# Chunk preparation of a delta-net kernel: loads one chunk ahead, the prompt chunk first, block inverses woven into the next group

## The chip, the core and the metric

The kernel runs on one core of one Trainium2 chip. A core has five engines that run side by side, each through its own instructions in order: TensorE (PE in the profile; the loading of its stationary operand is listed as PEld), VectorE (DVE), ScalarE (ACT), GpSimd (POOL) and SyncE (SP). SyncE issues most of the transfers; ScalarE and POOL issue some. All transfers run on the same 16 DMA engines. The metric is the device time of one execution in microseconds (us).

## The reference

One layer of a flow-matching backbone, for 128 prompt tokens and 2048 sample tokens of width 1024. Both groups go through the same steps, with other modulation vectors:

```
xn   = rmsnorm(h, ln_g) * (1 + scale) + shift
proj = xn @ w_in            # q,k,v | beta, decay | z_a | u_b v_b | z_b | x_c | z_c | 3 gates
A: q,k,v = silu(short_conv(qkv)); q,k normalised per head
   o = gated_delta(forward) + gated_delta(backward);  o_a = rmsnorm(o) * silu(z_a)
B: vs = w_spatial[g] @ rmsnorm(v_b) + b_spatial   per block of 128 tokens;  o_b = u_b * vs * silu(z_b)
C: o_c = real(fft over the token grid and channels of x_c) * silu(z_c)
merged = sum over n of sigmoid(gate_n) * (o_n @ w_branch[n])
y    = rmsnorm(h + gate * (merged @ w_out), final_g)
```

The gated delta rule is S_t = a_t (I - b_t k_t k_t^T) S_(t-1) + b_t k_t v_t^T with o_t = S_t^T q_t. It is computed by chunks: within a chunk a unit lower triangular matrix I + N, with N = beta * (k k^T) * decay, has to be inverted, and between chunks a state is carried. The final states of the prompt are an output as well.

## The kernel before

Activations lie in SBUF as `xh` and `xl`, two float16 parts of the normalised input, so a product with a weight takes three matmuls (`gemm_T`, `gemm_N`, all recorded under the helper's line L160). Weights are fetched with `getw`, whose second argument is how many further weights are requested at once: a request is a load of 512 KB on SyncE's queue (`wst`, L183), a sum of squares on ScalarE (L187), a broadcast of it by TensorE (`wscb` times `ones`, L170), and a split into `whi` and `wlo` (L189, L190).

The stages of the main line, in order: adaptive modulation and normalisation; 12 column tiles of q, k, v with the short convolution, each stored to DRAM as `qkv` (L509 and after); B's first part, 17 token tiles of `v_b` with its spatial product (L868 to L885), stored as `vs`; B's second part, 4 groups of columns of `u_b` and `z_b` (L888 to L898, with `gate_unit`, L835 to L849), each over 5 blocks of tokens; C, the Fourier branch, 4 groups (L911 to L968); then the merges of branches B, C and A, each with its gates, and the output projection.

Beside this main line runs the delta branch A as a Python generator, `delta()`. `Pace.tick` adds up the main line's matmul time and, for every 1.6 us of it, runs the generator up to its next `yield`. So the order of the instructions is written by this weaving, and a scheduler then places them on the engines. `delta()` first prepares the chunks, then runs the two scans (`scan_dir`, with `level`).

There are 17 chunks of 128 tokens; chunk 16 is the prompt. `prep` (L540 to L594) does one chunk in 7 steps: it loads q, k and v of all heads (`qr` and `kq`, L544), transposes them on TensorE (L546), normalises (L550 to L558), stores k and v (`kv`, L560), transposes k again to `T` (L564), loads the decay matrices (`dc`, L569), forms N for both directions (L577) and stores it (L583), cuts out its 32 x 32 diagonal blocks on POOL (`nd`, L579) and stores them (L585), and forms the q k^T product (L588 to L592).

The diagonal blocks of a group of chunks are inverted together by `base_inverse` (L596 to L633): 8 loads (L608), 31 pairs of VectorE operations (L616, L617), a split in two float16 parts, and 16 stores (`es` on L632, `ei` on L630). Before, the groups are chunks 0-3, 4-7, 8-11, 12-15 and 16 alone, and each group's inverse follows its last chunk. The scan's `level` loads what these stores wrote (`sn`, `ec`, `e3` on L639 to L643) and masks it on POOL (L649, L652).

Nearly all of these transfers are on SyncE's queue, in which an instruction that waits holds those behind it. The buffers `tok`, `qr`, `dc`, `T`, `XB`, `E` and `Et` exist once, `kq`, `nd` and `n` twice.

Of the kernel before, what the change touches and what calls it, by code (L numbers as in the profile page):

```python
# [15 lines left out]
ALU = mybir.AluOpType  # L16
# [94 lines left out]
def hybrid_flow_kernel(ctx: ExitStack, tc: tile.TileContext, x_prompt, x_sample, state_delta, c, c_ctx, ln_g, w_ada,  # L111
# [410 lines left out]
    GROUPS = [list(range(0, 4)), list(range(4, 8)), list(range(8, 12)), list(range(12, 16)), [16]]  # L522
# [11 lines left out]
    def h3(ap):  # L534
        return ap.rearrange("p (h x) -> p h x", h=H)

    def prep(g, ci, t):
        tok = sb(dq, [P, 2, WB], "tok")
        qr = sb(dq, [P, H, P], "qr")
        ss = sb(dq, [P, 2, H], "ss2", bufs=2)  # L540
        for part in range(3):
            ps = bank(ps_d, [P, WB])
            kq = qr if part == 0 else sb(dq, [P, H, P], "kq", bufs=2)
            SY.dma_start(kq, qkvD[part * 4:part * 4 + 4, :, chunk_off(t):chunk_off(t) + P].rearrange("h p t -> p h t"))  # L544
            for h in range(H):
                PE.transpose(ps[:, hs(h)], kq[:, h, :], ident)  # L546
            if part == 2:
                A.copy(tok[:, 1, :], ps)
                continue
            sq = sb(dq, [P, WB], "sq")  # L550
            A.activation(sq, ps, AF.Square)
            V.tensor_reduce(ss[:, part, :], h3(sq), AX.X, ALU.add)
            G.tensor_scalar(ss[:, part, :], ss[:, part, :], EPS, None, ALU.add)
            G.tensor_tensor(ss[:, part, :], ss[:, part, :], mhalf.to_broadcast([P, H]), ALU.pow)
            if part == 0:
                G.tensor_scalar(rq[:, t, :], ss[:, 0, :], P ** -0.5, None, ALU.mult)
            else:
                V.tensor_tensor(h3(tok[:, 0, :]), h3(ps), bc(ss[:, 1, :], P), ALU.mult)  # L558
            yield 1
        SY.dma_start(kvD[t], tok)  # L560
        T = sb(dq, [P, WB], "T")
        ps = bank(ps_d, [P, WB])
        for h in range(H):
            PE.transpose(ps[:, hs(h)], tok[:, 0, hs(h)], ident)  # L564
        A.copy(T, ps)
        A.dma_start(kTD[t], T)
        yield 1
        dc = sb(dq, [P, 2, WB], "dc")
        SY.dma_start(dc, decD[t])  # L569
        ps = bank(ps_d, [P, WB])  # L570
        for h in range(H):
            mm(ps[:, hs(h)], T[:, hs(h)], T[:, hs(h)])
        nd = sb(dq, [P, 2, H, 32], "nd", bufs=2)
        for d in range(2):
            n_ = sb(dq, [P, WB], "n32", bufs=2)
            for h in range(H):
                V.scalar_tensor_tensor(n_[:, hs(h)], ps[:, hs(h)], beta[:, d, t, h:h + 1], dc[:, d, hs(h)], ALU.mult, ALU.mult)  # L577
            for B in range(4):
                G.tensor_copy(nd[32 * B:32 * B + 32, d], h3(n_)[32 * B:32 * B + 32, :, 32 * B:32 * B + 32])  # L579
            n16 = sb(dq, [P, 2, WB], "n16", F16, bufs=2)  # L580
            A.activation(n16[:, 0, :], n_, AF.Copy, scale=FS)
            V.scalar_tensor_tensor(n16[:, 1, :], n_, FS, n16[:, 0, :], ALU.mult, ALU.subtract)
            SY.dma_start(nD[d][t], n16)  # L583
            yield 1
        SY.dma_start(ndD[g][:, :, ci].rearrange("d p h i -> p d h i"), nd)  # L585
        ps = bank(ps_d, [P, WB])
        for h in range(H):
            mm(ps[:, hs(h)], T[:, hs(h)], qr[:, h, :])  # L588
        for d in range(2):
            q_ = sb(dq, [P, WB], "n32", bufs=2)  # L590
            V.tensor_mul(q_, ps, dc[:, d, :])
            SY.dma_start(qkD[d][t], q_)  # L592
            yield 1

    def base_inverse(g):
        nt = len(GROUPS[g])  # L596
        nb = 4 * nt
        X = sb(dq, [P, 2048], "XB")[:, 0:1024]
        E = sb(dq, [P, 1024], "E")
        tmp = sb(dq, [P, 1024], "Et")  # L600
        if nt < 4:
            V.memset(X, 0.0)
            V.memset(tmp, 0.0)
        b3 = lambda t_: t_.rearrange("p (j i) -> p j i", j=32)
        blk = lambda t_, d, B: b3(t_[d * 64 + B * 16:d * 64 + B * 16 + nb, :])
        for d in range(2):
            for B in range(4):
                SY.dma_start(blk(X if d == 0 else tmp, d, B), ndD[g][d, 32 * B:32 * B + 32].rearrange("j t h i -> (t h) j i"))  # L608
        V.tensor_copy(b3(X[64:P, :]), tmp[64:P, :].rearrange("p (i j) -> p j i", j=32))
        G.memset(E, 0.0)  # L610
        G.memset(E[:, 0:1024:33], 1.0)
        X3, E3 = b3(X), b3(E)
        for k in range(31, 0, -1):
            n_ = 32 - k
            t3 = tmp[:, 0:k * n_].rearrange("p (j i) -> p j i", j=k)
            V.tensor_tensor(t3, X3[:, 0:k, k:k + 1].to_broadcast([P, k, n_]), E3[:, k:k + 1, k:32].to_broadcast([P, k, n_]), ALU.mult)  # L616
            V.tensor_tensor(E3[:, 0:k, k:32], E3[:, 0:k, k:32], t3, ALU.subtract)  # L617
            if k % 2 == 0:
                yield 1
        V.tensor_copy(b3(tmp), E.rearrange("p (i j) -> p j i", j=32))  # L620
        yield 1
        e16 = sb(dq, [P, 32, 2, 2, 32], "XB", F16)
        for w_, src in enumerate((E, tmp)):
            A.activation(e16[:, :, w_, 0, :], b3(src), AF.Copy, scale=FS)
            V.scalar_tensor_tensor(e16[:, :, w_, 1, :], b3(src), FS, e16[:, :, w_, 0, :], ALU.mult, ALU.subtract)
        yield 1
        for d in range(2):
            for B in range(4):
                p0_ = d * 64 + B * 16
                SY.dma_start(eD[g][d, 32 * B:32 * B + 32].rearrange("j t h c -> (t h) j c"),  # L630
                             e16[p0_:p0_ + nb].rearrange("p j w l c -> p j (w l c)"))
                SY.dma_start(e32D[g][d, 32 * B:32 * B + 32].rearrange("j t h c -> (t h) j c"), blk(E if d == 0 else tmp, d, B))  # L632
        yield 1  # L633

    def level(d, t):
        g = min(t // 4, 4)
# [179 lines left out]

    def delta():
        nonlocal dq
        for g, ts in enumerate(GROUPS):
            for ci, t in enumerate(ts):  # L820
                yield from prep(g, ci, t)
            yield from base_inverse(g)
        dl.close()
        dq = pool(dl, "dqb", 1, side="right")
        for d in range(2):
            V.tensor_tensor(eg[:, d], eg[:, d], rq, ALU.mult)
        for d in range(2):
            yield from scan_dir(d)
        dl.close()
        dps.close()  # L830
# [23 lines left out]
    bp = pool(bs, "bp", 2)  # L854
    bsp = sb(bp, [P, 4, P], "bsp", bufs=1)
    SY.dma_start(bsp, b_spatial[0].rearrange("g (o p) -> o g p", o=1).to_broadcast([P, 4, P]))
    vw = getw(4, 1)
    wsT = sb(bp, [P, 4, P], "wsT", bufs=1)
    wsn = sb(bp, [P, 4, P], "wsn", bufs=1)
    SY.dma_start(wsn, w_spatial[0].rearrange("g p q -> p g q"))  # L860
    ps = bank(ps_x, [P, 4, P])
    for g in range(4):
        PE.transpose(ps[:, g, :], wsn[:, g, :], ident)
# [4 lines left out]
    for t in range(NCH):  # L868
# [16 lines left out]
        SY.dma_start(vsD[:, :, t * P:(t + 1) * P].rearrange("g p t -> p g t"), vs)  # L885
        pace.tick(5.2)
    bs.close()
    for g in range(4):  # L888
        uw, zw = getw(2, 2)
        for ti, (t0, tn) in enumerate(TBS):  # L890
            st = sb(ep, [P, tn], "st", bufs=3)
            SY.dma_start(st, vsD[g][:, t0:t0 + tn])
            ps = bank(ps_mm, [P, tn])
            gemm_T(ps, uw, 0, xh[:, :, t0:t0 + tn], xl[:, :, t0:t0 + tn])
            with tc.high_priority():
                V.scalar_tensor_tensor(st, ps, uw.inv, st, ALU.mult, ALU.mult)
            pace.tick(tn / 100)
            gate_unit(1, g, ti, zw, st)  # L898


    fs = ExitStack()
    fp = pool(fs, "fp", 1)
    cf = sb(fp, [P, _CW - _CF], "cf")
    SY.dma_start(cf, consts[:, _CF:_CW])
    for n_, (a, b) in _COFF.items():
        if a >= _CF:
            K[n_] = cf[:, a - _CF:b - _CF]
# [3 lines left out]
    for g in range(4):  # L911
        xw, zw = getw(2, 2)
        for gh in range(1):
            yT = sb(fp, [P, NTOK], "yT", bufs=1)
            Y1 = sb(fp, [P, 64, 32], "Y1")
            for q in range(0, NCH, 4):
# [13 lines left out]
                else:  # L930
# [1 line left out]
                    mm(ps, xc[:, 0, :], K["dftcs"])  # L932
                    yp = sb(fp, [P, 2 * P], "yp")
                    V.tensor_copy(yp, ps)
# [222 lines left out]
```

## Time and profile before

| what | value |
|---|---|
| device time, median of 3 runs | 2378.42 us (2374.1 to 2380.57) |
| profiled execution: device time | 2377.82 us |
| profiled execution: span | 2376.0 us |
| mean granted TensorE clock | 0.981 |
| TensorE busy | 2261.1 us (95%) |
| VectorE busy | 1271.6 us (54%) |
| ScalarE busy | 765.0 us (32%) |
| POOL busy | 820.9 us (35%) |
| moved by DMA | 350.40 MB, mean 147 GB/s |

The profile is that of one execution. Busy times are per engine and overlap each other. Rows of waits read "engine, operation and its line, what it waited for: total us, how often, the longest". SPq is SyncE's queue, whose rows are the issues of transfers and not the transfers. The granted clock (PEclk) is the speed that TensorE was given, as a share of full speed. In a group of instructions, "out<-in" names tiles without their buffer numbers; a `b` is a PSUM bank. "+15 forms" says that instructions of other shapes are in the same group.

### The profile page before, as it was taken

The numbers are of one execution on the slowest core, as the hardware profiler recorded it, in microseconds if no ns is written. First come the engines' busy times: TensorE is split into PE (matmuls) and PEld (weight loads), VectorE is DVE, ScalarE is ACT, GpSimd is POOL, SyncE is SP. The second block draws the span as 40 slices with busy tenths as digits, with TensorE's granted clock in tenths as the row PEclk, the third lists the DMA queues.
The fourth block names the chain that finished last, engine by engine and source line by source line (L and its number), as shares of the span: only waits on it lengthen the run. The fifth ranks groups of instructions, "written<-read, shape, count | busy, mean of one in ns | idle before, by whom it ended". The sixth has DMA issues, their size and how long they took to land. (4 is left out here: it accounts for less than half of the span.)

```text
span 2376.0 us, 43430 instructions
## 1 busy us (share of the span) xinstructions
PE 2261.1 (95%) x17092; PEld 1376.6 (58%) x17092; DVE 1271.6 (54%) x3117; ACT 765.0 (32%) x1430; POOL 820.9 (35%) x1056
## 2 busy tenths in 40 slices
PE   7999899998989987899989999999999999999998
PEld 3554444798545676679656656656665444444443
DVE  5635743568575856655574556674654242332453
ACT  3444543322333332332332222242332242221331
POOL 2421122342434431345423233445552212122543
PEclk9999999999999998999999999999999999999999
DMA  8315632375857672244453445565563253332542
GB/s 278 129 50 174 226 110 76 109 254 132 241 138 237 190 181 58 82 139 131 138 181 124 129 138 158 162 201 178 160 182 109 95 163 119 113 97 80 189 151 98
DMA packets 353238, 350.40 MB, mean 147 GB/s; under 512 B 70929, under 2 KB 273674, under 8 KB 351498
## 3 DMA queue, kind: packets, MB, share of 16 engines
q1 hardware_dynamic: 338986, 294.13, 41.9%
q0 software_dynamic: 9152, 40.13, 4.3%
q10 hardware_dynamic: 4896, 13.37, 1.5%
q8 instruction: 134, 2.20, 0.4%
q14 instruction: 70, 0.57, 0.1%
HBM read 222.16 MB, written 125.39 MB: 146 GB/s over the span
## 5 line engine op out<-in xcount | busy, mean ns | idle before, releaser
L160 PE MATMUL b<-xh,whi 128*128 128x512 f16 (+1 forms) x2080 | 707.2, 350 | 18.5 <-ACT raw L500 11.6
L160 PE MATMUL b<-xl,whi 128*128 128x512 f16 (+1 forms) x2080 | 708.5, 350 | 0.1
L160 PE MATMUL b<-xh,wlo 128*128 128x512 f16 (+1 forms) x2080 | 707.8, 350 | 0.0
L160 PEld LDWEIGHTS <-whi 128*128 128x128 f16 x4160 | 389.9, 98 | 402.0 <-issue 36.3
L160 PEld LDWEIGHTS <-wlo 128*128 128x128 f16 x2080 | 204.4, 98 | 195.8 <-issue 9.8
L160 PE MATMUL b<-big,bhi 128*128 128x512 f16 (+1 forms) x960 | 252.8, 348 | 5.7 <-ACT big L987 4.2
L1019 POOL TENSOR_TENSOR mrow<-mrow,sg 128x512 f32<-128x512 f32 (+1 forms) x80 | 87.9, 1102 | 317.0 <-DVE sg L1018 237.3
L160 PE MATMUL b<-whi,xh 128*128 128x128 f16 x1088 | 191.7, 222 | 0.6 <-DVE sg L844 0.5
L160 PE MATMUL b<-whi,xl 128*128 128x128 f16 x1088 | 191.8, 222 | 0.0
L160 PE MATMUL b<-wlo,xh 128*128 128x128 f16 x1088 | 191.8, 222 | 0.0
L160 PEld LDWEIGHTS <-xh 128*128 128x128 f16 x2312 | 179.5, 99 | 6.6 <-issue 5.8
L1009 ACT ACTIVATE sg<-b,winv 128x512 f32<-128x512 f32 (+1 forms) x120 | 74.6, 621 | 305.4 <-PE b L160 296.9
L160 PE MATMUL b<-big,blo 128*128 128x512 f16 (+1 forms) x480 | 163.8, 348 | 0.0
L1018 DVE SCALAR_TENSOR_TENSOR sg<-b,binv,sg 128x512 f32<-128x512 f32 (+1 forms) x80 | 53.5, 669 | 182.6 <-PE b L160 180.6
L752 POOL TENSOR_SCALAR skn<-skn,ed 128x128 f32<-128x128 f32 x136 | 80.5, 607 | 180.4 <-DMA skn<-kv 164.6
L160 PEld LDWEIGHTS <-bhi 128*128 128x128 f16 x960 | 89.2, 98 | 84.2 <-ACT big L987 2.4
L509 POOL TENSOR_TENSOR cy<-cy,raw 128x545 f32<-128x545 f32 (+1 forms) x48 | 55.4, 1180 | 223.6 <-ACT raw L508 223.6
L160 PEld LDWEIGHTS <-xl 128*128 128x128 f16 x1224 | 115.0, 99 | 0.4
L652 POOL TENSOR_TENSOR R<-ec,cst 128x512 f16<-128x512 f16 x68 | 72.6, 1088 | 103.6 <-PE b L160 50.5
L160 PE MATMUL b<-wohi,mh 128*128 128x512 f16 x272 | 104.2, 383 | 2.2 <-ACT mh L1064 2.2
L160 PE MATMUL b<-wohi,ml 128*128 128x512 f16 x272 | 104.1, 384 | 2.0 <-DVE ml L1065 2.0
L160 PE MATMUL b<-wolo,mh 128*128 128x512 f16 x272 | 104.2, 383 | 0.0
(369 smaller groups left out, 3714.9 us busy)
## 6 DMA issues: line engine op xcount, KB each, us to landing
wst<-in_w_in_dram SPq DMA_DIRECT2D x60, 512.0 KB
qkv<-cy POOLq DMA_DIRECT2D x12, 1089.0 KB, 4.5
mrow<-br SPq DMA_DIRECT2D x24, 512.0 KB
mrow<-mrg SPq DMA_DIRECT2D x19, 512.0 KB
mrow<-mrg SPq DMA_DIRECT2D x16, 576.0 KB
mrg<-mrow POOLq DMA_DIRECT2D x16, 576.0 KB, 3.2
dc<-dec SPq DMA_DIRECT2D x17, 512.0 KB
kq<-qkv SPq DMA_DIRECT2D x34, 256.0 KB
```

The costliest lines, as they stand in the source:

```text
L160: PE.matmul(out, l, r, start=start, stop=stop)
L509: G.tensor_tensor(y[:, c0:c1], y[:, c0:c1], raw[:, 1 + c0:1 + c1], ALU.mult)
L652: G.tensor_tensor(dst[:, l].rearrange("p h a b c -> p h (a b) c"), wide(ec[:, :, which ^ d, l, :]), bm, ALU.mult)
L752: G.tensor_scalar(kn_[:, hs(h)], kn_[:, hs(h)], ed[:, d, t, h:h + 1], None, ALU.mult)
L1009: A.activation(sg, ps, AF.Sigmoid, scale=gw.inv)
L1018: V.scalar_tensor_tensor(sg, ps, binv[:, 1:2], sg, ALU.mult, ALU.mult)
L1019: G.tensor_tensor(mr, mr, sg, ALU.add)
```

## The change

The order of the chunks becomes 16, then 0 to 15, with groups [16], 0-3, 4-7, 8-11, 12-15. `prep` no longer loads its own inputs: a dictionary `held` carries the k, v and q rows and the decay matrices of the next chunk, which each `prep` requests when its own last reader of that buffer has been issued. The order of the parts becomes k, v, q. The inverse of a group is stepped along with the preparation of the group after it, in five of each `prep`'s seven steps, and has five steps without work after its loads. The last group's inverse runs by itself, before the scans. The stores of `kv` and `nd` go from SyncE's queue to POOL's.

In the main line, B's spatial weights are requested before its first four weights. In B's second part, a whole row of `vs` (2176 tokens, 1.1 MB) is loaded for each group, one group ahead, in place of five blocks. The Fourier constants `cf` (640 KB) are loaded on ScalarE's queue instead of SyncE's. The second matrix product of the prompt's Fourier transform comes after the first of the four blocks of the sample's transform instead of before it.

```diff
-    GROUPS = [list(range(0, 4)), ..., list(range(12, 16)), [16]]
+    GROUPS = [[16], list(range(0, 4)), ..., list(range(12, 16))]
...
+    def rows(part, t):
+        x = sb(dq, [P, H, P], "kq" if part else "qr", bufs=2 if part else 1)
+        SY.dma_start(x, qkvD[part * 4:part * 4 + 4, :, chunk_off(t):chunk_off(t) + P].rearrange("h p t -> p h t"))
+        return x
...
-    def prep(g, ci, t):
+    def prep(g, ci, t, nxt, held):
...
+        cur = dict(held)
...
+        def more(key, make):
+            if nxt is not None:
+                held[key] = make()
+
+        ps = turned(1)
+        norm(ps, 1)
+        V.tensor_tensor(h3(tok[:, 0, :]), h3(ps), bc(ss[:, 1, :], P), ALU.mult)
+        yield 1
+        A.copy(tok[:, 1, :], turned(2))
+        more(1, lambda: rows(1, nxt))
+        norm(turned(0), 0)
+        G.tensor_scalar(rq[:, t, :], ss[:, 0, :], P ** -0.5, None, ALU.mult)
+        yield 1
+        G.dma_start(kvD[t], tok)
...
+        more(2, lambda: rows(2, nxt))
         yield 1
-        dc = sb(dq, [P, 2, WB], "dc")
-        SY.dma_start(dc, decD[t])
+        dc, qr = cur["dc"], cur[0]
...
-        SY.dma_start(ndD[g][:, :, ci].rearrange("d p h i -> p d h i"), nd)
+        G.dma_start(ndD[g][:, :, ci].rearrange("d p h i -> p d h i"), nd)
...
             SY.dma_start(qkD[d][t], q_)
+            if d:
+                more(0, lambda: rows(0, nxt))
+                more("dc", lambda: decay_rows(nxt))
             yield 1
...
     def base_inverse(g):
...
+        for _ in range(5):
+            yield 0
...
     def delta():
...
-        for g, ts in enumerate(GROUPS):
-            for ci, t in enumerate(ts):
-                yield from prep(g, ci, t)
-            yield from base_inverse(g)
+        seq = [(g, ci, t) for g, ts in enumerate(GROUPS) for ci, t in enumerate(ts)]
+        held = {1: rows(1, 16), 2: rows(2, 16), 0: rows(0, 16), "dc": decay_rows(16)}
+        yield 1
+        base = iter(())
+        for i_, (g, ci, t) in enumerate(seq):
+            if ci == 0 and g:
+                for r_ in base:
+                    if r_:
+                        yield 1
+                base = base_inverse(g - 1)
+            for n_, _ in enumerate(prep(g, ci, t, seq[i_ + 1][2] if i_ < 16 else None, held)):
+                yield 1
+                if n_ % 7 not in (2, 5) and next(base, 0):
+                    yield 1
+        for r_ in base:
+            if r_:
+                yield 1
+        for _ in base_inverse(4):
+            yield 1
...
-    vw = getw(4, 1)
     wsT = sb(bp, [P, 4, P], "wsT", bufs=1)
     wsn = sb(bp, [P, 4, P], "wsn", bufs=1)
     SY.dma_start(wsn, w_spatial[0].rearrange("g p q -> p g q"))
+    vw = getw(4, 1)
...
+    vnext = sb(vp, [P, NTOK], "vrow")
+    SY.dma_start(vnext, vsD[0])
     for g in range(4):
         uw, zw = getw(2, 2)
+        vrow = vnext
+        if g < 3:
+            vnext = sb(vp, [P, NTOK], "vrow")
+            SY.dma_start(vnext, vsD[g + 1])
         for ti, (t0, tn) in enumerate(TBS):
-            st = sb(ep, [P, tn], "st", bufs=3)
-            SY.dma_start(st, vsD[g][:, t0:t0 + tn])
+            st = vrow[:, t0:t0 + tn]
...
-    SY.dma_start(cf, consts[:, _CF:_CW])
+    A.dma_start(cf, consts[:, _CF:_CW])
...
                     V.tensor_copy(yp, ps)
-                    ps = bank(ps_x, [P, P])
-                    mm(ps, K["dftcs"][:, 0:P], yp[:, 0:P], True, False)
-                    mm(ps, K["dftms"], yp[:, P:2 * P], False, True)
-                    A.copy(yT[:, NS:NTOK], ps)
...
                 pace.tick(3.5)
+                if q4 == 0:
+                    ps = bank(ps_x, [P, P])
+                    mm(ps, K["dftcs"][:, 0:P], yp[:, 0:P], True, False)
+                    mm(ps, K["dftms"], yp[:, P:2 * P], False, True)
+                    A.copy(yT[:, NS:NTOK], ps)
```

More of the change, by code (lines that the diff above doesn't have):

```diff
@@ L521, in hybrid_flow_kernel @@
     oss = [sb(cp, [P, 20], f"oss{n}") for n in range(3)]
-    GROUPS = [list(range(0, 4)), list(range(4, 8)), list(range(8, 12)), list(range(12, 16)), [16]]
+    GROUPS = [[16], list(range(0, 4)), list(range(4, 8)), list(range(8, 12)), list(range(12, 16))]
     ndD = [dram(f"nd{g}", [2, P, len(ts), H, 32]) for g, ts in enumerate(GROUPS)]
@@ L535, in h3, with turned @@
         return ap.rearrange("p (h x) -> p h x", h=H)
-    def prep(g, ci, t):
+    def rows(part, t):
[3 more added lines that the diff above has]
+    def prep(g, ci, t, nxt, held):
         tok = sb(dq, [P, 2, WB], "tok")
-        qr = sb(dq, [P, H, P], "qr")
         ss = sb(dq, [P, 2, H], "ss2", bufs=2)
-        for part in range(3):
+        cur = dict(held)
+        def turned(part):
@@ L542, in prep @@
             ps = bank(ps_d, [P, WB])
-            kq = qr if part == 0 else sb(dq, [P, H, P], "kq", bufs=2)
-            SY.dma_start(kq, qkvD[part * 4:part * 4 + 4, :, chunk_off(t):chunk_off(t) + P].rearrange("h p t -> p h t"))
             for h in range(H):
[L546 to L549, printed above, removed]
+                PE.transpose(ps[:, hs(h)], cur[part][:, h, :], ident)
+            return ps
@@ L550, in prep, with norm @@
+        def norm(ps, i):
             sq = sb(dq, [P, WB], "sq")
             A.activation(sq, ps, AF.Square)
[L552 to L558, printed above, removed]
@@ L559, in prep @@
-            yield 1
-        SY.dma_start(kvD[t], tok)
+            V.tensor_reduce(ss[:, i, :], h3(sq), AX.X, ALU.add)
+            G.tensor_scalar(ss[:, i, :], ss[:, i, :], EPS, None, ALU.add)
+            G.tensor_tensor(ss[:, i, :], ss[:, i, :], mhalf.to_broadcast([P, H]), ALU.pow)
+        def more(key, make):
[4 more added lines that the diff above has]
+        V.tensor_tensor(h3(tok[:, 0, :]), h3(ps), bc(ss[:, 1, :], P), ALU.mult)
@@ L635, in level @@
     def level(d, t):
-        g = min(t // 4, 4)
+        g = 0 if t == 16 else 1 + t // 4
         ci = t - GROUPS[g][0]
@@ L898, in hybrid_flow_kernel @@
             gate_unit(1, g, ti, zw, st)
+    vst.close()
     fs = ExitStack()
```

6 lines of the change are left out of this document (added).

## The prediction

> **What bounds the kernel now.** I read the head of the page and its chain first, then the stages, then TensorE's waits in the stages that the change touches. The page:
>
> ```profile
> span 2376.0 us, 43430 instructions
> ...
> PE 2261.1 (95%) x17092; PEld 1376.6 (58%) x17092; DVE 1271.6 (54%) x3117; ACT 765.0 (32%) x1430; POOL 820.9 (35%) x1056
> ...
> PE 6%; POOL 0%; DMA 0%; DVE 0%; ACT 0%; issue 0%; DVEq 0%; POOLq 0%; ACTq 0%; SPq 0%
> ```
>
> TensorE is busy 2261.1 of 2376.0 us. The chain reaches back only 6% of the span and names the tail, which the change leaves alone; so it cannot price this edit, and what counts is TensorE's idle time and clock, stage by stage. The windows (columns: window, length, busy time of each engine with its instructions, granted clock, DMA share, GB/s) are B's first part, two halves of B's second part, the Fourier branch up to the first scan step, its rest, and all after it:
>
> ```profile
> 460.00:600.00 140.00, 129.98 (x1756) 121.31 (x1753) 101.43 (x271) 38.66 (x77) 56.75 (x116) 0.99 0.66 193
> 600.00:720.00 120.00, 107.23 (x611) 57.91 (x610) 72.60 (x179) 37.78 (x69) 44.99 (x75) 0.96 0.72 200
> 720.00:890.00 170.00, 158.95 (x1258) 110.18 (x1257) 110.53 (x271) 60.09 (x117) 66.60 (x117) 0.97 0.70 197
> 890.00:1000.00 110.00, 88.96 (x942) 72.28 (x940) 72.27 (x171) 29.33 (x61) 23.84 (x29) 0.91 0.31 76
> 1000.00:1190.00 190.00, 187.55 (x2109) 153.31 (x2107) 106.66 (x291) 60.09 (x159) 91.24 (x107) 1.00 0.44 132
> 1190.00:2376.00 1186.00, 1155.60 (x7666) 636.17 (x7664) 563.73 (x1452) 335.34 (x630) 422.15 (x459) 0.99 0.45 141
> ```
>
> The first four rows hold all chunk preparations and block inverses. Idle there: 10.0 + 12.8 + 11.0 + 21.0 = 54.9 us before 1000, and 2.5 us after. The clock is lowest in the same rows (0.91 in the worst). So at most 55 us of idle and some 18 us of slow clock (each row's shortfall of clock times its busy time: 1 + 4 + 5 + 8) can be won. TensorE's waits between 460 and 1000 (total, times, longest) name that idle time:
>
> ```profile
> PE b L160 <- DVE yp L934: 8.5, 1, 8.5
> PE b L546 <- DMA qr<-qkv: 7.1, 3, 6.3
> PE b L160 <- DMA skn<-kv: 7.1, 1, 7.1
> PE b L160 <- DVE sg L844: 6.6, 2, 6.1
> PE b L160 <- DVE wscb L170: 4.4, 2, 3.0
> PE b L546 <- DVE n L577: 4.0, 3, 1.9
> PE b L160 <- DVE sg L879: 3.0, 1, 3.0
> PE b L863 <- DMA wsn<-in_w_spatial_dram: 2.0, 1, 2.0
> PE b L564 <- DVE tok L558: 1.9, 3, 1.1
> ```
>
> **The change, part by part.** TensorE's own work is unchanged, so every term is a wait.
>
> *Loads one chunk ahead.* SyncE's queue shows why a load came late. After a group's inverse it issues 16 stores, and the next chunk's loads stand behind them:
>
> ```profile
> 695.20 2.38 SPq L632 DMA_DIRECT2D es<-E  x4
> 697.68 3.58 SPq L632 DMA_DIRECT2D es<-Et  x4
> 701.36 7.66 SPq L630 DMA_DIRECT2D ei<-XB  x8
> 709.07 0.70 SPq L569 DMA_DIRECT2D dc<-dec  x1
> ```
>
> From 695.20 to 709.07 nothing else leaves the queue. The dc load comes out at 709.07, VectorE waits for it, and TensorE waits for the gate product behind that (the 6.1 us of L844). The 6.3 us for qr is the same thing one burst later. In the compiled order of the changed kernel the loads of the next chunk (dc, kq, qr) stand ahead of each burst. Both stalls go: 6.1 + 7.1 (all three qr waits) = 13.2 us. They also cost clock:
>
> ```profile
> 712.00:725.00 13.00, 9.22 (x34) 3.95 (x34) 6.54 (x16) 3.28 (x7) 4.52 (x11) 0.74 1.06 328
> 845.00:857.00 12.00, 7.20 (x84) 7.13 (x85) 2.06 (x3) 2.48 (x4) 2.75 (x5) 0.72 0.81 232
> ```
>
> The lost work is 0.26 x 9.2 + 0.28 x 7.2 = 4.4 us by these two rows. Together 17.6 us.
>
> *The inverse woven into the next group, with five yields after its loads.* The 3.0 us before L879 is VectorE standing at L609 for the Et load (rows below, 4.06 us); five empty steps put TensorE work ahead of it, so it goes. Of the rows n L577 and tok L558, 5.9 us together, I take half, 3 us: their cause is preparation work crowding VectorE beside the inverse, which is spread and not removed. Ends: 0 and 5.9.
>
> *Spatial weights requested before B's v weights.* The 2.0 us at L863 goes; the v weights follow some half a microsecond later, under a stage whose first matmuls wait for neither (ends: -1 and +2 us of gain). Sum so far: 17.6 + 3.0 + 3 + 2.0 = 25.6.
>
> *Whole rows of B.* Twenty loads L892 become four of 1.1 MB. VectorE waited for the old ones, but TensorE had other work:
>
> ```profile
> DVE st L896 <- DMA st<-vs: 11.8, 7, 4.6
> ```
>
> The gain on the path is put at 0 (ends: 0 and 3). The cost: the first two rows stand on SyncE right after the last vs store, with the next weight load wst behind them. Before, that load came out here, late by the burst ahead of it, and TensorE's 3.0 us on wscb followed:
>
> ```profile
> 596.65 0.45 SPq L904 DMA_DIRECT2D cf<-in_consts_dram  x1
> 597.20 8.33 SPq L630 DMA_DIRECT2D ei<-XB  x8
> 605.63 0.75 SPq L183 DMA_DIRECT2D wst<-in_w_in_dram  x1
> ```
>
> The burst moves away from this place and 2.2 MB of transfer takes it. At the 200 GB/s of the 600:720 row that is 11 us, at the highest that a window here shows (328) 7 us. I leave the 3.0 us where it is: 0 (ends: a gain of 3, a loss of 4).
>
> *Fourier constants from ScalarE.* Before, cf came out at 596.65, far ahead of the Fourier window. In the changed order it stands behind the first xc copy on ScalarE, one group before use; what TensorE does in between hides part of it. Ends: 0, and 4 us (640 KB at 328 GB/s is 2.0 us, and as much again where the queues are full). I take 1 us of loss, nearer to the bare transfer.
>
> *Stores of kv and nd from POOL.* 34 issues leave SyncE and join POOL, where one takes 0.6 us:
>
> ```profile
> 673.12 0.60 POOL L848 DMA_DIRECT2D br<-st  x1
> ```
>
> That is 20 us of POOL, idle 65% of the time: 0, and what it costs without that cover is the second rival. *Postponing the prompt's second Fourier matmul* removes the place where TensorE stood 8.5 us; but VectorE was late there because of the lone inverse of chunk 16, so this belongs to the next part.
>
> *The last inverse.* Before, chunk 16 was last with an inverse of its own, and 890:1000 lost 21.0 us idle and, at 0.91, about 8 us of clock (0.09 x 89). Now the last group is 12 to 15; its inverse has no later chunk to be woven into and stands alone. Its length by rows of before:
>
> ```profile
> 525.58 1.06 PE L160 MATMUL b<-qr,T 128*128 128x128 f32 x8
> 542.98 1.03 DVE L609 COPY XB<-Et 64x1024 f32<-64x1024 f32 x1 [4.06 <-DMA Et<-nd]
> 660.58 1.05 DVE L609 COPY XB<-Et 64x1024 f32<-64x1024 f32 x1 [3.40 <-DMA dc<-dec]
> L617 DVE TENSOR_TENSOR E<-E,Et 128x31 f32<-128x31 f32 (+15 forms) x62 | 25.0, 403 | 1.5
> L616 DVE TENSOR_TENSOR Et<-XB,E 128x31 f32<-128x31 f32 (+15 forms) x62 | 22.8, 367 | 3.4 <-DMA XB<-nd 2.0
> 974.87 1.96 SPq L632 DMA_DIRECT2D es<-E  x4
> 995.80 0.21 PE L160 MATMUL b<-T,sn 128*128 128x64 f16 x1 [7.08 <-DMA skn<-kv]
> ```
>
> The last qr,T product to the first inverse operation: 542.98 - 525.58 = 17.4 us. The inverse: two of them took 25.0 + 22.8 us of pure VectorE time, 23.9 each; with the stage's other VectorE work between, the second group's ran from 660.58 to its first store at 695.20, 34.6 us. Its end to the first scan product, through 16 stores, the scan's loads and POOL's mask products: 995.80 - 974.87 = 20.9. Together 73 us. In the compiled order of the changed kernel, TensorE has about 54 us of work between those two products (its matmuls there at the durations of before). So it stalls some 19 us at the scan's start, with perhaps 4 us of other waits and 6 us of slow clock (estimates: half the clock loss and a fifth of the idle time that the row of before has): 29 us against 29 before. The part comes out at 0 (ends: a gain of 21, if nothing idles there any more; a loss of 15, with the chain at 88 us).
>
> The steps of the delta work grow from 209 to some 215 (five more in the lone inverse, one at the start), at 1.6 us of TensorE work each 10 us; the scan begins earlier by more than that (37 us of TensorE work, by the two orders), so no merge gets its input later: 0.
>
> Sum: 25.6 - 1.0 = 24.6. The profiled execution took 2377.82 us (span 2376.0 and 1.8 around it), 0.6 under the median of 2378.42. 2377.8 - 24.6 = 2353.2, and against the median 2353.8: I write 2353.
>
> **Rivals.**
>
> *One: the lone inverse eats the gain.* The chain from the last preparation to the scan is 88 us instead of 73 (the inverse at twice its pure time, 48 us, as on a VectorE that is half taken, and 2 more for its stores), so the stall is 34 and the part loses 15, with 4 of the vs row burst: 2353 + 19 = 2372, inside 0.3%. For it: 7.1 us of skn wait already stands at this place. Against: the postponed Fourier product takes 8.5 us out.
>
> *Two: POOL becomes the bound, and the kernel is slower.* The kv store waits for tok; that wait moves from SyncE, where it held only loads, to POOL, where the gate products and the mean-square steps stand behind it. The wait in the profile:
>
> ```profile
> SPq L560 <- DVE tok L558: 33.8, 9, 10.9
> ```
>
> 33.8 / 9 = 3.8 us each; over 17 chunks 64 us. POOL's own operations already stretch when VectorE is busy (minimum, median, maximum):
>
> ```profile
> L579 POOL COPY nd<-n x16: 279/287/2002, 860.9 to 887.1; 32x128 f32<-32x128 f32 x16
> ```
>
> If half of the 64 reaches TensorE, the time is 2353 + 32 = 2385. It decides from 25 / 3.8, some seven chunks, on. Against: the store stands one step (1.6 us of TensorE work) behind the copies that it waits for, and the gate has three st and four sg buffers. The Trainium skill, "SBUF — State Buffer", section "Who interferes with whom", speaks for this rival: a DMA issued from POOL needs descriptors that POOL cannot write while VectorE holds their shared port, and it names ScalarE's or SyncE's queue as the cure, the reverse of this edit. The trace agrees as to POOL's copies (287 ns grows to 2002); that a store is delayed no row shows.
>
> *Three: the scan's start is covered too.* The 21 us idle there go entirely, as the scan's loads find free queues, and with them some clock: 2353 - 25 = 2328. For it: the 1000:1190 row, with scan steps woven into Fourier work, idles only 2.5 us. Against: the 54 us above.
>
> *Four: nothing changes.* The stalls at L844 and L546 were taken in place of other waits (the DMA share is 1.06 and 0.81 there), and the loads, though asked for sooner, land no sooner: 2353 + 18 = 2371. Against it: 709.07 is the issue, not the landing.
>
> **How the numbers follow.** Forecast 0.50; one 0.13; two 0.19; three 0.11; four 0.07. What a measurement of this kernel tells from no change is about 0.3%, 7 us, so faster means below 2371. The forecast and three are faster, with some of one and four (0.07): 0.68. The rest of these two is no change, 0.13; two is slower, 0.19. The forecast's own range, from the ends of its terms (3 of weaving, 4 of cf and wst, up to 10 of the scan's start either way, not all together), is 2340 to 2366. For 8 in 10 it reaches to 2328, the third rival, and to 2384, leaving out about half of the second.
>
> **What would show it.** Right: no wait on qr at L546 and none over 2 us on the gate product in B's second part; the dc and qr issues ahead of each burst of 16; the idle time of the B rows down from 34 to under 15 us; a wait of 15 to 25 us at the first T,sn product; a wscb wait near the first u group; yp no longer named. Wrong: that wait above 30 us (one); POOL's waits on tok with st and sg waits of TensorE behind them (two); the same L546 and L844 waits with an early issue (four).

## The result and the profile after

The changed kernel takes 2363.31 us (median of 5; 2358.12 to 2364.54) against 2378.42: a ratio of 0.9937, 95% interval 0.992 to 0.9955, about 15 us. The forecast was 2353. The profiled execution after is the one of 2363.31 us. Its page:

```profile
span 2361.5 us, 43403 instructions
...
PE 2255.3 (96%) x17092; PEld 1376.8 (58%) x17092; DVE 1264.6 (54%) x3117; ACT 763.2 (32%) x1430; POOL 846.9 (36%) x1090
```

The span fell by 14.5 us: TensorE's idle time from 114.9 to 106.2 (span less busy time), its busy time by 5.8 with the same 17092 matmuls. To see where, the span is cut at the same places of the main line in both kernels: the start of B's first part, of its second part, of the Fourier branch, and of the merges. The columns are those of the prediction's windows. Before:

```profile
0.00:473.20 473.20, 443.47 (x2938) 235.77 (x2939) 250.23 (x498) 206.08 (x325) 121.96 (x168) 0.98 0.43 144
473.20:585.80 112.60, 108.71 (x1519) 104.54 (x1520) 81.96 (x223) 30.24 (x64) 42.15 (x94) 0.98 0.63 187
585.80:825.20 239.40, 219.30 (x1373) 126.04 (x1372) 155.84 (x387) 80.56 (x148) 98.77 (x161) 0.97 0.71 201
825.20:1185.40 360.20, 329.40 (x3582) 272.01 (x3579) 216.57 (x556) 110.74 (x263) 135.86 (x177) 0.96 0.45 123
1185.40:2376.00 1190.60, 1160.18 (x7687) 638.20 (x7687) 566.99 (x1456) 337.33 (x633) 422.15 (x459) 0.99 0.45 142
```

After:

```profile
0.00:471.90 471.90, 441.30 (x2928) 234.47 (x2929) 250.72 (x493) 205.57 (x324) 121.81 (x166) 0.99 0.43 145
471.90:591.50 119.60, 110.49 (x1529) 105.89 (x1530) 89.92 (x246) 31.32 (x66) 50.30 (x104) 0.98 0.62 183
591.50:838.10 246.60, 226.02 (x1428) 134.90 (x1427) 176.56 (x452) 82.52 (x152) 116.06 (x196) 0.95 0.72 205
838.10:1207.90 369.80, 350.65 (x3922) 291.94 (x3922) 212.89 (x560) 115.26 (x288) 163.37 (x202) 0.98 0.47 133
1207.90:2361.50 1153.60, 1126.86 (x7287) 609.62 (x7287) 534.48 (x1368) 328.57 (x601) 395.40 (x423) 0.99 0.44 139
```

| stage | idle before, us | idle after, us | clock before | clock after |
|---|---|---|---|---|
| up to B | 29.7 | 30.6 | 0.98 | 0.99 |
| B, first part | 3.9 | 9.1 | 0.98 | 0.98 |
| B, second part | 20.1 | 20.6 | 0.97 | 0.95 |
| Fourier branch | 30.8 | 19.2 | 0.96 | 0.98 |
| merges and output | 30.4 | 26.7 | 0.99 | 0.99 |

Three stages became longer and the last one 37.0 us shorter: the delta branch runs earlier, so 400 matmuls (7687 to 7287) left the merges. Lengths of stages therefore say nothing here, and idle time does. B, where the forecast had most of its gain, idles 5.7 us more than before. The Fourier branch, where it had one wait on qr (6.3 us at 849.80) and otherwise zero, idles 11.6 us less at a better clock. Two of its waits account for that. Before (825.2 to 1185.4):

```profile
PE b L160 <- DVE yp L934: 9.0, 2, 8.5
PE b L546 <- DMA qr<-qkv: 6.7, 2, 6.3
```

After (838.1 to 1207.9), yp is in no row, and qr has:

```profile
PE b L551 <- DMA qr<-qkv: 1.8, 1, 1.8
```

The 8.5 us on yp were VectorE standing at the start of chunk 16's own inverse, in the kernel before:

```profile
921.15 8.44 SPq L630 DMA_DIRECT2D ei<-XB  x8
...
932.74 0.91 DVE L602 MEMSET XB<- 128x1024 f32 x1 [7.39 <-DMA Et<-nd]
...
939.49 0.42 DVE L934 COPY yp<-b 128x256 f32<-128x256 f32 x1
```

That inverse follows directly on the one of chunks 12 to 15, and `XB` exists once: its clearing (L602) stood 7.4 us, by the profile for the Et loads, which left the queue behind the ei stores of the inverse before, and the copy of yp came 6.75 us after it began.

TensorE's waits of the changed kernel from 440 to 1010:

```profile
PE b L551 <- DMA qr<-qkv: 10.2, 2, 8.4
PE b L160 <- DVE sg L918: 7.7, 3, 4.5
PE b L160 <- DMA skn<-kv: 7.7, 1, 7.7
PE b L551 <- DVE n L591: 4.1, 2, 3.0
PE b L160 <- DVE wscb L170: 3.9, 1, 3.9
PE b L160 <- ACT xc L972: 3.1, 2, 1.8
PE b L902 <- DMA wsn<-in_w_spatial_dram: 2.6, 1, 2.6
PE b L160 <- DMA cf<-in_consts_dram: 2.0, 1, 2.0
```

The 6.1 us on the gate product (now L883) are down to 0.4, and the 8.5 us on yp are gone. The wait on qr is larger than before, and so is that on the normalised v (now L918). The next views of the changed kernel show why. SyncE's queue and TensorE around the qr wait:

```profile
744.19 2.21 SPq L656 DMA_DIRECT2D es<-E  x4
746.50 4.43 SPq L656 DMA_DIRECT2D es<-Et  x4
751.03 7.62 SPq L654 DMA_DIRECT2D ei<-XB  x8
758.75 1.39 SPq L539 DMA_DIRECT2D qr<-qkv  x1
...
764.86 1.09 PE L551 MATMUL b<-cst,qr 128*128 128x128 f32 x4 [8.39 <-DMA qr<-qkv]
```

Asked for one chunk ahead, qr is still late: there is one qr buffer, so its load comes only after the product that reads the old contents (the qr,T product at 748.97 in the trace), and by then the 16 stores are in the queue. The longest wait on the normalised v, 4.5 us up to 589.84, comes behind VectorE's stand at the start of an inverse:

```profile
583.94 1.08 DVE L633 COPY XB<-Et 64x1024 f32<-64x1024 f32 x1 [7.38 <-DMA dc<-dec]
```

Why VectorE stands at L633 is plainer at a later inverse, with POOL, SyncE and VectorE:

```profile
778.53 3.50 POOL L593 COPY nd<-n 32x128 f32<-32x128 f32 x8 [5.13 <-DVE n L591]
782.32 0.74 POOL L599 DMA_DIRECT2D nd<-nd  x1 [0.30 <-POOL nd L593]
785.66 2.73 SPq L630 DMA_DIRECT2D XB<-nd  x4
788.43 3.79 SPq L630 DMA_DIRECT2D Et<-nd  x4
795.04 1.05 DVE L633 COPY XB<-Et 64x1024 f32<-64x1024 f32 x1 [6.17 <-DMA Et<-nd]
```

The blocks go from POOL's copies through DRAM and eight loads to VectorE in 13 us after the store's issue, and VectorE, which takes its instructions in order, stands at L633 for 6.2 of them. Five empty steps did not hide this round trip.

The scan's start is as long as worked out, and better filled. The window from the last qr,T product to the first scan product, and the two ends of its last part:

```profile
867.90:940.40 72.50, 61.00 (x651) 49.07 (x650) 48.03 (x115) 20.57 (x42) 15.98 (x23) 0.96 0.45 99
...
917.67 2.22 SPq L656 DMA_DIRECT2D es<-E  x4
...
940.43 0.21 PE L160 MATMUL b<-T,sn 128*128 128x64 f16 x1 [7.66 <-DMA skn<-kv]
```

The window is 72.5 us long, where the prediction had 73; but TensorE was busy in 61.0 of them and not in 54, and idled 11.5, with 7.7 at the scan product.

### The profile page after: what moved, and what is told of

Read it like the earlier page. It is cut to its first block, busy times and chain, and to the rows that moved or that the text cites. A ratio compares the mean times of both kernels' runs of the same rounds, so it can differ in the third digit from the quotient of the medians.

```text
span 2361.5 us, 43403 instructions
## 1 busy us (share of the span) xinstructions
PE 2255.3 (96%) x17092; PEld 1376.8 (58%) x17092; DVE 1264.6 (54%) x3117; ACT 763.2 (32%) x1430; POOL 846.9 (36%) x1090
## 5 line engine op out<-in xcount | busy, mean ns | idle before, releaser
L160 PE MATMUL b<-xh,whi 128*128 128x512 f16 (+1 forms) x2080 | 706.4, 349 | 13.4 <-ACT raw L500 11.5
```

Source lines behind the costliest of these rows:

```text
L160: PE.matmul(out, l, r, start=start, stop=stop)
```

## The experiments

All ratios are to the kernel before, run on the same chip beside the experiment. Medians of one kernel differ by some microseconds from chip to chip (before: 2378.4 to 2381.1), so ratios are compared, with their 95% intervals.

### One part alone, on the kernel before

Loads only: the new `prep` with all else as before. (The five empty steps stand in this kernel too, but its loop passes over them.)

```diff
+    def rows(part, t): ...
+    def decay_rows(t): ...
-    def prep(g, ci, t):
+    def prep(g, ci, t, nxt, held):
...
+            if ci == len(GROUPS[g]) - 1:
+                for r_ in base_inverse(g):
```

> The kernel before with only the loads of a chunk asked for one chunk ahead (and k, v, q in that order): chunk order, inverses after their group, stores, rows of B, constants, spatial weights and the prompt's Fourier product as before. Theory A (the late loads carried the gain): 2378 - 13 - 4 = 2361 us, no wait on qr over 2 us, no 6 us wait on the gate product at L844, and the 8.5 us at yp still there. Rival B (the weaving of the inverses carries it): 2373 to 2378 us, with the gate product or qr still late behind the 16 stores.

Measured: 1.0009 (0.9995 to 1.0024). No gain. TensorE's waits of that kernel, 455 to 1200:

```profile
PE b L160 <- DVE yp L964: 12.2, 2, 6.8
PE b L551 <- DVE n L591: 8.8, 5, 4.8
PE b L551 <- DMA qr<-qkv: 6.0, 1, 6.0
```

The two 6 us waits of before are not gone together: the one on the gate product (here L874) is down to 3.3, qr has its 6.0, its load again coming out right behind a burst of stores (805.20 to 819.71), and n and yp grew. My first theory, that late loads by themselves carried the gain, falls here. No run undoes the loads on the changed kernel, so whether the gain needs them is not shown.

The order of the chunks alone:

```diff
-    GROUPS = [list(range(0, 4)), ..., list(range(12, 16)), [16]]
+    GROUPS = [[16], list(range(0, 4)), ..., list(range(12, 16))]
```

> The kernel before with the order of the chunks alone changed (16 first, then 0 to 15; the inverse of 12 to 15 last), nothing else. Theory A (the order is worth by itself what its undoing cost, some 8 us: an inverse fewer stands at the scan's start): 2367 to 2372 us, idle in the Fourier branch 19 us or less instead of 29, yp under 2 us. Rival B (the order is worth something only with inverses stepped along and loads ahead): 2376 to 2380 us.

Measured: 0.9988 (0.9976 to 1.0001), nothing that stands out. Yp is still waited for there. Around its copy (943.09) VectorE runs the inverse of chunks 12 to 15 without a pause, from 930 to 945:

```profile
PE b L160 <- DVE yp L934: 5.9, 2, 5.3
```

Whole rows of B alone:

```diff
+    vnext = sb(vp, [P, NTOK], "vrow")
+    SY.dma_start(vnext, vsD[0])
...
-            SY.dma_start(st, vsD[g][:, t0:t0 + tn])
+            st = vrow[:, t0:t0 + tn]
```

> The kernel before with whole rows of B in place of the 20 block loads, nothing else (the constants' load then waits for the rows' space on SyncE's queue). Theory A (the block loads hold SyncE, since each waits for an st buffer that a stored gate product still occupies, and everything behind them is late; undone, 15.5 us of such waits came back and 10 us of time): 2366 to 2371 us, and waits on qr and on L844 down. Rival B (they hold SyncE only where loads one chunk ahead stand behind them; alone, the rows delay the weights and constants as much): 2376 to 2382 us.

Measured: 1.0007 (0.9996 to 1.0017), nothing. So no one of these three gains by itself.

### One part undone, on the changed kernel

The changed kernel's own ratio is 0.9937 (0.992 to 0.9955). First the 20 block loads of B:

```diff
-            st = vrow[:, t0:t0 + tn]
+            st = sb(ep, [P, tn], "st", bufs=3)
+            SY.dma_start(st, vsD[g][:, t0:t0 + tn])
```

> The changed kernel with B's 20 loads of a block each in place of the four whole rows. Theory A (rows are worth nothing on the path, and cost the 3.9 us on wscb and the 2 us on cf, whose space is the rows' and free only after them): 2357 to 2363 us, both waits under 1 us. Rival B (rows relieve VectorE, SyncE and the DMA engines in B's second part, a part of the gain): 2367 to 2372 us, VectorE waiting 10 us or more for st again.

Measured: 0.9978 (0.9965 to 0.9991). The intervals are apart: within the changed kernel the rows are worth about 0.0041 x 2378 = 10 us, which I had put at nothing. What SyncE's queue waited for in this kernel (600 to 850), and TensorE (455 to 1200):

```profile
SPq L931 <- DMA br<-st: 15.5, 3, 8.4
```

```profile
PE b L551 <- DMA qr<-qkv: 16.3, 2, 8.8
```

A block load needs one of three `st` buffers, which the gate products use too; where the product's store (`br`) has not left the buffer, SyncE stands, 8.4 us at the longest, and what is behind it waits. In the kernel before, the same wait is smaller (580 to 850):

```profile
SPq L892 <- DMA br<-st: 4.8, 2, 3.1
```

That these stands cost the 10 us is not shown. The two long ones end at 671.75 and 802.25, and TensorE has no wait over 1.4 us in the 20 us after either; its waits on qr end at 772.24 and 874.59, each for a load that came out behind a burst of stores (767.16 and 868.48), as in the changed kernel. As theory A of this run said, the wait on cf is gone without the rows; the one on wscb (4.1 us) is not. VectorE waits 18.3 us for st again, as rival B said, and the time is rival B's direction and past its end.

The chunk order undone, all else as changed:

```diff
-    GROUPS = [[16], list(range(0, 4)), ..., list(range(12, 16))]
+    GROUPS = [list(range(0, 4)), ..., list(range(12, 16)), [16]]
```

> The changed kernel with the chunks and groups in the old order (0 to 15, then 16 alone), all else as changed: the inverse of 12 to 15 is stepped along with chunk 16 only and then run out, and chunk 16's own inverse follows alone. Theory A (the order carries the gain, because before the prompt's inverse of a quarter of the blocks costs VectorE and SyncE as much as a full one and stood in front of the scan): TensorE idles 26 to 30 us in the Fourier branch instead of 19, the first scan product is 40 us later, 2373 to 2378 us. Rival B (the weaving, wherever the prompt stands, carries it): 2363 to 2367 us.

Measured: 0.9966 (0.9952 to 0.9979), some 7 us worse, and its interval just overlaps the changed kernel's. By the ratio (0.9966 of 2378) that is 2370 us, between the two theories. The place is not theory A's. Its Fourier branch:

```profile
851.00:1200.50 349.50, 332.00 (x3688) 273.66 (x3688) 209.93 (x562) 107.35 (x266) 140.91 (x170) 0.98 0.39 113
```

It idles 17.5 us there, no more than the changed kernel's 19.2, and yp is in no row, though VectorE still stands 6.4 us at the start of the lone prompt inverse (L624, at 918.62). So with all else changed, the order is not needed for the gain in the Fourier branch. The profiled execution idles more elsewhere: 27.2 us in B's second part, where the changed kernel has 20.6, and 35.2 ahead of B instead of 30.6.

The weaving undone, each inverse run after its group:

```diff
-                if n_ % 7 not in (2, 5) and next(base, 0):
-                    yield 1
...
+            if ci == len(GROUPS[g]) - 1:
+                for r_ in base_inverse(g):
+                    if r_:
+                        yield 1
```

> The changed kernel with each inverse run alone after its group, the prompt's chunk still first. Theory A (loads ahead carry most, weaving half of 6 us of crowding): 2363 + 3 to 2363 + 8 us. Rival B (weaving carries the gain, since it gives VectorE and SyncE time between the parts of an inverse): 2375 us or more. Rival C (weaving is nothing, or costs, because it puts the 16 stores in the middle of a chunk, ahead of its qr load): 2355 to 2363 us, and the qr wait of 8.4 us gone.

Measured: 0.9964 (0.995 to 0.9979), some 6 us worse, the intervals again just touching. The time is theory A's, 2370 us by the ratio; its place is not, since B and the Fourier branch idle no more than in the changed kernel. The Fourier branch:

```profile
824.40:1185.00 360.60, 347.00 (x3883) 288.02 (x3884) 224.54 (x596) 116.41 (x283) 166.75 (x218) 0.99 0.50 142
```

It idles 13.6 us, less than the changed kernel's 19.2, at a clock of 0.99, and waits 0.2 us on yp. So with all else changed, the stepping along of the inverses is not needed for the gain in the Fourier branch either. What this execution has more is in the merges: 38.3 us of idle time against 26.7. Among its waits from 1200 on, where the sums of the modulation's last third run on VectorE:

```profile
PE b L160 <- DVE st L305: 11.7, 4, 3.9
```

The changed kernel has 3.7 us of it (1207 to 2360). Why these sums come later without the weaving stays open.

The prompt's second Fourier product put back:

```diff
-                if q4 == 0:
-                    ps = bank(ps_x, [P, P])
...
                     V.tensor_copy(yp, ps)
+                    ps = bank(ps_x, [P, P])
...
```

> The changed kernel with the prompt's second Fourier product back in its old place, before the first of the four blocks. Theory A (the 8.5 us wait on yp was VectorE, late from the lone inverse of chunk 16 ahead of it; without it the place costs nothing): 2361 to 2366 us, yp under 2 us. Rival B (the postponing took the wait out, and is the gain in the Fourier branch): 2370 to 2374 us, with 5 to 9 us on yp in one or more of the four groups.

Measured: 0.9946 (0.9926 to 0.9965), as the changed kernel. In the old place yp now costs 0.5 us:

```profile
PE b L160 <- DVE yp L982: 0.5, 1, 0.5
```

So the 8.5 us are gone without the moving of the product. They are gone as well without the stepping along (0.2 us) and with the chunks in the old order (no row), while the loads alone keep 12.2 us and the order alone 5.9. So none of these three parts (moving, stepping along, order) is needed for it by itself, and the order alone is not enough; which of them are enough together is open.

The kv and nd stores back on SyncE:

```diff
-        G.dma_start(kvD[t], tok)
+        SY.dma_start(kvD[t], tok)
...
-        G.dma_start(ndD[g][:, :, ci]...)
+        SY.dma_start(ndD[g][:, :, ci]...)
```

> The changed kernel with the kv and nd stores back on SyncE's queue. Theory A (the move to POOL is free, as predicted): 2360 to 2366 us, the same as the changed kernel. Rival B (POOL became an in-order bound: the 7.7 us on the normalised v in B's first part, and VectorE's 16 us on vss, come from POOL's stores): 2353 to 2356 us, and these waits at or below 3 us. Rival C (SyncE's queue is what limits, and the move is part of the gain): 2368 to 2373 us.

Measured: 0.9943 (0.9922 to 0.9964), the same. Within these intervals, some 5 us, the move is free either way. The wait on the normalised v is not POOL's doing; with the stores on SyncE it is larger, and its longest (up to 589.34) comes behind 9.1 us of VectorE at L633 (587.73):

```profile
PE b L160 <- DVE sg L918: 11.3, 3, 8.4
```

### Taking the remaining waits away

Two buffers of qr:

```diff
-        x = sb(dq, [P, H, P], "kq" if part else "qr", bufs=2 if part else 1)
+        x = sb(dq, [P, H, P], "kq" if part else "qr", bufs=2)
```

> The changed kernel with two buffers of qr instead of one. Theory A (the 8.4 us wait of TensorE on qr at 764.86, and 1.8 at 863, are there because the one qr buffer is freed only by the last product of the chunk before, and the load is then queued behind the 16 stores of an inverse on SyncE): the two waits go, and with them about 2 us of slow clock in 750 to 768; 2363 - 12 = 2351 us, qr no longer among TensorE's waits. Rival B (the wait only hides the next one: the k rows, dc or the gate product behind the same 16 stores are late instead): 2360 to 2364 us, and another wait of 6 us or more stands at the same place.

Measured: 0.992 (0.9899 to 0.9941): at most a few us better than the changed kernel, not told apart from it. The qr wait of 10.2 us is gone, so its cause was the buffer. The gain is not there, because the next thing is late:

```profile
792.49 1.06 DVE L633 COPY XB<-Et 64x1024 f32<-64x1024 f32 x1 [11.34 <-DMA Et<-nd]
```

```profile
PE b L578 <- DVE tok L567: 8.9, 4, 4.8
```

TensorE, no longer held by qr, runs ahead to the point where VectorE stands 11.3 us for the inverse's blocks, and waits 4.8 us for tok behind it (at 800.26). Rival B comes nearest, with other names and a longer wait at this place.

Two buffers of qr and the eight es stores of each inverse on ScalarE's queue:

```diff
-                SY.dma_start(e32D[g][d, 32 * B:32 * B + 32]...
+                A.dma_start(e32D[g][d, 32 * B:32 * B + 32]...
```

> Two buffers of qr, and the eight es stores of each inverse on ScalarE's queue, so that eight and not sixteen stores stand on SyncE. Theory A (SyncE's bursts are what the remaining waits have in common): the scan's loads come out 6 us sooner, the wait at the first scan product falls from 6.9 to 2 us or less, the other waits after bursts (tok, n, wscb) halve; 2350 to 2356 us. Rival B (the waits that are left are VectorE's, behind the 62 operations of an inverse): 2360 to 2364 us with two qr or without. Rival C (ScalarE stands at the stores, and sigmoids come late): 2366 us or more.

Measured: 0.991 (0.989 to 0.9929), 2359.71 us, the fastest of all, though its interval overlaps the changed kernel's. The first scan product still waits:

```profile
915.53 7.53 SPq L654 DMA_DIRECT2D ei<-XB  x8
...
932.65 0.21 PE L160 MATMUL b<-T,sn 128*128 128x64 f16 x1 [6.15 <-POOL T L676]
```

The ei stores, which need the split of the inverse first, come out at 915.53 and take 7.5 us as ever. From the end of the inverse's last column on VectorE (911.6) to the scan product it is 21.0 us without the es stores on SyncE, and 22.8 in the changed kernel (917.6 to 940.43). Theory A had a wait of 2 us there and loads 6 us sooner, and was wrong about what this length consists of. By the ratio the time is 2357 us, between theory A and rival B.

The steps of the inverse spaced otherwise, on the changed kernel:

```diff
-        for _ in range(5):
+        for _ in range(9):
             yield 0
...
-            if k % 2 == 0:
+            if k % 3 == 0:
                 yield 1
...
-                if n_ % 7 not in (2, 5) and next(base, 0):
+                if next(base, 0):
```

> The changed kernel with the inverse's steps spaced otherwise: nine empty steps after its loads and not five, ten steps of three columns and not fifteen of two, in all seven steps of a preparation, so that its stores come well ahead of the next inverse's loads. Theory A (VectorE stands at L633 because an inverse's block loads come out behind the last one's 16 stores; 18 us in all, and what TensorE waits for next, normalised v, n and tok, follows from it): L633 waits under 5 us in all, 2353 to 2357 us. Rival B (VectorE's 62 operations themselves make the rest late): 2361 to 2368 us, n, tok or gate products late by as much.

Measured: 0.9982 (0.9969 to 0.9994), slower than the changed kernel by some 11 us, and outside both theories. VectorE's waits of this kernel, 460 to 1000:

```profile
DVE XB L633 <- DMA Et<-nd: 20.7, 4, 9.5
DVE XB L633 <- DMA vs<-vs: 7.0, 1, 7.0
```

The changed kernel has:

```profile
DVE XB L633 <- DMA Et<-nd: 10.6, 2, 6.2
DVE XB L633 <- DMA dc<-dec: 7.4, 1, 7.4
```

That is 27.7 us at L633 against 18.0. The longest of these waits, 9.5 us at 697.39, has its loads at 688.74, 39 us after the last store of the inverse before left the queue (649.65): the theory that the loads queue behind the stores falls, and what is left, argued from the rows around 782 above, is the round trip of the blocks through DRAM, which nine empty steps did not cover either. The profiled execution (2366) is the fastest of its runs, so it does not show where the median's 2375 comes from.

The same spacing with two qr buffers and es on ScalarE:

> The same spacing with two qr buffers and the es stores on ScalarE's queue. Theory A (the three causes are apart: one qr buffer, eight more stores on SyncE, block loads behind stores): 2346 to 2352 us, no wait over 3 us in B's second part. Rival B (each of them only uncovers the next): 2356 to 2361 us, as with two of them.

Measured: 0.995 (0.9933 to 0.9968), 2367 us. Rival B is the nearer one, but even it expected less time: with the other two edits in, the spacing costs some 9.5 us, and what is left is not told apart from the changed kernel.

## Why the time held and the mechanism did not

The time, the direction and the range held: 2363 against 2353 with a range of 2328 to 2384. That is luck for the most part. The waits in which the forecast saw its gain (gate product, qr, normalised v, n, tok, spatial weights), with the cost on cf, came out 3.4 us longer in all instead of some 20 us shorter, and the gain arose where the forecast had put next to nothing. Of its signs of being right, those on the gate product and on yp held, and a wait on wscb came (3.9 us, at 648.55). Four did not hold: qr is waited for, the bursts at 744 and 842 stand ahead of the qr load, B idles more instead of less, and the first scan product waits 7.7 us and not 15 to 25. By its own steps:

- *Loads one chunk ahead, 17.6 us: half wrong.* The wait on L844 (6.6 us) is down to 0.4. The waits on qr went from 7.1 to 10.2 us: the 6.3 at 849.80 became 1.8 at 863.05, and 8.4 are new at 764.86. The step that failed reads "the loads of the next chunk (dc, kq, qr) stand ahead of each burst". For qr this does not hold at the burst of 744, since its single buffer is freed late. The slow clock went along with the wait: 0.77 from 750 to 768. Alone, the loads are worth nothing (1.0009).
- *Five yields take the 3.0 us before L879 away: wrong.* It is 7.7 us now. The stand at L633 went on, and 27.7 us with nine yields show that empty steps do not remove it.
- *Half of n and tok, 3 us: the size was wrong.* They went from 4.0 and 1.9 us to 4.1 and 1.0, by 0.8 in all.
- *Spatial weights, 2.0 us: wrong.* The wait is 2.6 us.
- *Whole rows at nothing: wrong in this kernel.* Undone, they cost 10 us; by themselves they are worth nothing (1.0007), so the price goes with the rest of the change. By which wait they cost it stays open.
- *wscb stays at 3.0, cf costs 1: about right;* 3.9 and 2.0.
- *Stores on POOL at nothing: right,* shown by their undoing. The rival of POOL as the bound is out. The Trainium skill, "SBUF — State Buffer", section "Who interferes with whom", spoke for it; these runs do not agree as to the time, since 34 stores from POOL beside a busy VectorE cost nothing that can be told (0.9937 with them, 0.9943 without).
- *The lone last inverse at nothing: wrong by its second half.* The chain, 73 us, was right to 1 us. TensorE had 61 us of work beside it and not 54, so it idled 11.5 us and not 19; and yp's 8.5 us did not come back. In the Fourier branch 11.6 us of idle time went, and the clock rose from 0.96 to 0.98, about 7 us of its 350 busy; in B's second part it fell from 0.97 to 0.95, some 5 us of 226 the other way.
- *The earlier scan at nothing: roughly right.* The merges idle 3.7 us less. The prediction's "2.5 us after" 1000 ends at 1190; the merges idled 30.4 us before.

So by the profiled executions the gain lies in the Fourier branch, where VectorE no longer holds TensorE at yp and qr is waited for less, and not in a B without stalls. Which part of the change brings it is not isolated. It stays for the most part when the order, the stepping along or the moving of the product is undone by itself (17.5, 13.6 and 22.1 us idle there, against 30.8 before). The kernels with the loads alone and the order alone idle 25.4 and 22.8 us there with no gain that stands out, so this idle time by itself does not price the change. How much of the 15 us each part carries is not settled. The parts do not add: none of three gains alone, and the undoing of any one of order, weaving and rows loses 6 to 10 us of 15, for order and weaving with intervals that just touch the changed kernel's, and with the loss in other stages than the Fourier branch. The loads, the spatial weights and the queue of cf were never undone.

## What to carry to other kernels

A load that is asked for earlier comes earlier only if its buffer is free earlier: count the buffers before counting the gain, and look in the queue for what stands ahead of it at that moment (here one qr buffer, and 8.4 us). Where several waits follow each other on one in-order engine, taking one away moves the stall to the next, so that parts of an edit can be worth nothing alone and much together; test by undoing as well as by doing. A buffer that is shared between loads and results makes the loading queue wait for the results' stores (15.5 us in the kernel with block loads); look for it among the queue's own waits, and do not take it for lost time before TensorE is seen to wait behind it.

## What the runs showed that I had not expected

The same 17092 matmuls kept TensorE busy for 2255.3 us (changed) and 2261.1 (before), and idle time alone accounts for 8.7 of the 14.5 us. The other 5.8 us need not be the change's: the traces of the loads alone and of the rows alone, which gain nothing, have 2256.0 us busy. Executions of one kernel spread by up to 16 us: the respaced kernel ran from 2366.16 to 2382.59, and the one with the order alone from 2368.3 to 2383.08, so one trace need not show what the median does. And the es stores, 8 of the 16 of an inverse, moved to a second queue, shortened the way from the inverse's end to the first scan product by little, from 22.8 to 21.0 us: the ei stores alone still hold SyncE for 7.5 us.
